# The Fourier stage of an encoder trunk, feature transform first: from transposed input through a transpose on TensorE to the token transform

## The chip, the cores and the metric

The kernel runs on one core of a Trainium2 chip. Its engines are TensorE (PE; PEld is its weight load), VectorE (DVE), ScalarE (ACT), GpSimd (POOL) and SyncE (SP, which here only issues DMAs). The metric is the device time of one execution in microseconds (us); lower is better. The profile is one execution taken by the hardware profiler; "span" is the time from its first to its last instruction.

## What is computed

Two sequences of 512 tokens and 1024 features go through the same two layers. The part that matters is the token mixer of layer 0, a Fourier mixing over tokens and, in eight groups of 128, over features:

```python
def rms_norm(x, g):
    x32 = x.astype(jnp.float32)
    y = x32 * lax.rsqrt(jnp.mean(x32 * x32, axis=-1, keepdims=True) + EPS)
    return (y * g.astype(jnp.float32)).astype(x.dtype)

def fourier_mix(h, w_out):
    B, S, _ = h.shape
    hg = h.astype(jnp.float32).reshape(B, S, N_FGROUPS, F_GROUP)
    f = jnp.fft.fft2(hg, axes=(1, 3), norm="ortho").real
    f = f.reshape(B, S, D_MODEL).astype(h.dtype)
    return f @ w_out
...
x = x + fourier_mix(rms_norm(x, fourier_norm[j]), fourier_w_out[j])
```

The real part of the two-dimensional transform is cosine times cosine minus sine times sine. Behind it, layer 0 has a squared-ReLU MLP, layer 1 has attention and another MLP, and a final norm ends the trunk; none of that is touched.

## The kernel before

**Precision.** Every matmul operand is split into a rounded part (hi, float32r) and the rest (lo). `split` (L80) does it with a cast on ACT and a subtraction on DVE (or POOL), `split_scaled` (L84) with a scale on the way. `mm3` (L75) makes a product from three matmuls: hi·hi, hi·lo, lo·hi (lines L76, L77 and L78 of the profile).

**Buffers.** All large tiles share 38 slots of 4 KB a partition (`slot`), eight of 2 KB (`tm`), five raw load buffers (`rawp`), four weight pairs (`wp`) and the eight PSUM banks (`ps`). The order of all five queues in the Fourier stage is the order of the calls in the program (`manual_schedule`): an instruction that waits holds up everything behind it on its own engine.

**The Fourier stage before.** Each input comes twice: as `x` by tokens ([token, feature], tokens and features folded so that mirrored ones lie together) for the transform, and as `xt` transposed for the residual. Per sequence:

- `Front` (L325) takes two of the four token tiles: sum of squares on ACT, gain on DVE (L339), sum and difference of mirrored features (`plus`, `minus`), root of the norm, scale by it, fold of mirrored tokens (`combine`), split. `mask` and row 0 carry token 256, which has no mirror.
- `transform` (L443) runs the token transform first (`seq_part`, L403: cosine and sine tables as the moving operand, 258 or 256 columns), evacuates and splits it (`seq_evac`), and then the feature transform (`feat_stage`, L419). The middle feature (64 of a group) goes beside it: 8-row operands (`seq_nyq`, `nyqT`), and the alternating row for token 256 is a product with one row (L395, L396).
- `even_outs` and `odd_outs` (L518 to L538) multiply the two halves of the result by folded output weights, four tiles `we` and four tiles `wo`, made by `Fold` (L462: plus, minus, even, odd) and, for the middle features, `FoldNyq`. Each output group is 12 matmuls, in the even half with one more for the middle features (L532).

The order (L578 on): Front of sequence 0, its transform with the weight folds on POOL in between, loads of the next `x`, then even and odd outputs of sequence 0 while Front of sequence 1 runs. As `xt` of sequence 0 isn't yet needed, `Aside` (L551) copies these outputs off by ACT and adds them to `xt` later, on POOL and DVE, during sequence 1's transform. Then come the outputs of sequence 1, added at once (`even_add`, `odd_add`), beside which the next stage begins: squares and gains of sequence 0 (`finish`), its root, and the first MLP weights.

**The lines of the steps.** `sums` (L156) adds squares over the partitions by float32 matmuls against a tile of ones (L160); `spread` and `tokens` show a float32 transpose on TensorE (L168, L1344). `rsqrt_steps` (L121) is a chain of seven small steps over DVE and ACT.

Of the kernel before, what the change touches and what calls it, by code (L numbers as in the profile page):

```python
# [11 lines left out]
F32 = mybir.dt.float32  # L12
# [6 lines left out]
P = 128  # L19
D = 1024  # L20
# [19 lines left out]
def trunk_kernel(ctx, tc, x_in, xt_in, y_out, dcos, dsin, feat, rope, gfour, gcol, grow, gfin,  # L40
# [215 lines left out]
    xa = {}  # L256

    def load_x(q, t):
        xa[q, t] = slot([P, D], F32)
        nc.sync.dma_start(xa[q, t], x_in[q][t * P : (t + 1) * P, :])  # L260

# [11 lines left out]
    def begin():  # L273
        gr = slot([P, D], F32)
        nc.sync.dma_start(gr, gfour.to_broadcast([P, D]))
        load_x(0, 0)
        load_x(0, 1)
        rcos = table(dcos, 3 * 258)
        load_x(0, 2)
        load_x(0, 3)  # L280
        rsin = table(dsin, 512)
        rft = table(feat, 846)
        gc = cons.tile([P, 4 * KC], F32, name="gc")
        nc.sync.dma_start(gc, gcol)
        return gr, rcos, rsin, rft, gc
# [11 lines left out]
    gr, rcos, rsin, rft, gc = begin()  # L297
    tabs = [slot([P, D], F32R) for _ in range(2)]
    cosT = [t[:, :516].rearrange("p (a b) -> p a b", a=2) for t in tabs]
    altT = tabs[0][0:1, 516:774]  # L300
    pickT = tabs[1][:, 516:594]
    sinT = slot([P, 2, 512], F32R)
    fslot = slot([P, D], F32R)
    ft = fslot[:, :512].rearrange("p (a b) -> p a b", a=2)
    nyqT = fslot[0:8, 512:1024]

    def table_cos():
        for c in range(2):
            split(cosT[c][:, 0], cosT[c][:, 1], rcos[:, c * 258 : (c + 1) * 258])
        nc.scalar.copy(altT, rcos[0:1, 516:774])  # L310
# [4 lines left out]
    def table_feat():  # L315
        split(ft[:, 0], ft[:, 1], rft[:, :256])
        nc.scalar.copy(nyqT, rft[0:8, 334:846])
        nc.scalar.copy(pickT, rft[:, 256:334])
# [4 lines left out]
    ee, oo, ny = {}, {}, {}  # L323

    class Front:  # L325


        def __init__(self, q, c):
            self.q, self.c = q, c
            self.ss, self.r = small(2), small(2)  # L330
            self.steps = rsqrt_steps(self.r[:, :2], self.ss[:, :2], 2, 1.0 / D)
            self.xg, self.p, self.m = [None] * 2, [None] * 2, [None] * 2

        def squares(self, i):
            sumsq(xa[self.q, 2 * self.c + i], self.ss[:, i : i + 1])

        def gain(self, i):
            self.xg[i] = slot([P, D], F32)
            nc.vector.tensor_mul(self.xg[i], xa[self.q, 2 * self.c + i], gr)  # L339

        def plus(self, i):
            self.p[i] = tm()
            nc.vector.tensor_add(self.p[i], self.xg[i][:, :512], self.xg[i][:, 512:])

        def minus(self, i):
            self.m[i] = tm()
            nc.vector.tensor_sub(self.m[i], self.xg[i][:, :512], self.xg[i][:, 512:])

        def chain(self, a, b):
            for step in self.steps[a:b]:  # L350
                step()
            if b == 7 and self.c == 0:
                self.rm = small(1)
                nc.vector.tensor_mul(self.rm[:, :1], self.r[:, 1:2], mask)

        def scale(self):
            for x in (self.m[0], self.p[0]):
                nc.scalar.activation(x, x, AF.Copy, scale=self.r[:, 0:1])

        def combine(self):  # L360
            (p1, p2), (m1, m2), r, w = self.p, self.m, self.r, 8
            stt = nc.vector.scalar_tensor_tensor
            n32 = sm.tile([P, 16], F32, tag="n32", name=nm("n32"), bufs=2)
            n = sm.tile([P, 2, 16], F32R, tag="ny", name=nm("ny"), bufs=4)


            rr = r[:, 1:2]
            if self.c == 0:
                rr, w = self.rm[:, :1], 16
                nc.vector.tensor_scalar(n32[:, 8:16], m2[:, 0:512:64], r[:, 1:2], None, ALU.mult)  # L370
            stt(n32[:, 0:8], m2[:, 0:512:64], rr, m1[:, 0:512:64], ALU.mult, ALU.add)
            stt(p1, p2, rr, p1, ALU.mult, ALU.add)
            stt(m2, m2, r[:, 1:2], m1, ALU.mult, ALU.subtract)
            split(n[:, 0, :w], n[:, 1, :w], n32[:, :w])
            ny[self.q, self.c] = n

        def split_even(self):
            e = slot([P, 2, 512], F32R)
            split(e[:, 0], e[:, 1], self.p[0])
            ee[self.q, self.c] = e  # L380

        def split_odd(self, eng=nc.vector):
            o = slot([P, 2, 512], F32R)
            if self.c == 0:
                nc.scalar.activation(self.m[1][0:1, :], self.p[1][0:1, :], AF.Copy, scale=self.r[0:1, 1:2])
            split(o[:, 0], o[:, 1], self.m[1], eng)
            oo[self.q, self.c] = o

        def split(self, eng=nc.vector):
            self.split_even()  # L390
            self.split_odd(eng)

    def seq_even(o, lhs, alt, c):
        if c == 1:
            nc.tensor.matmul(o, alt[0], altT, start=False, stop=False)  # L395
            nc.tensor.matmul(o, alt[1], altT, start=False, stop=False)  # L396
        mm3(o, lhs[0], lhs[1], cosT[c][:, 0], cosT[c][:, 1], c == 0, c == 1)

    def seq_nyq(q, c, o):
        seq_even(o[0:8, :258], [ny[q, c][:, i, 0:8] for i in range(2)],  # L400
                 [ny[q, 0][0:1, i, 8:16] for i in range(2)], c)

    def seq_part(q, j, c, o, v):  # L403
        js = slice(j * P, (j + 1) * P)
        seq_even(o[:, :258], [ee[q, c][:, i, js] for i in range(2)],
                 [oo[q, 0][0:1, i, js] for i in range(2)], c)
        cs = slice(c * 256, (c + 1) * 256)
        mm3(v[:, :256], oo[q, c][:, 0, js], oo[q, c][:, 1, js],
            sinT[:, 0, cs], sinT[:, 1, cs], c == 0, c == 1)

    def seq_evac(o, v):
        a, b = slot([P, 2, 258], F32R), tm((P, 2, 256), F32R)
        split(a[:, 0], a[:, 1], o[:, :258])
        split(b[:, 0], b[:, 1], v[:, :256])
        return a, b
# [3 lines left out]
    def feat_stage(q, j, a, b, an, en):  # L419
        u, v = ps(), ps()  # L420
        mm3(u[:, :258], ft[:, 0, 0:P], ft[:, 1, 0:P], a[:, 0], a[:, 1], True, False)
        nyt = nyqT[:, j * P : (j + 1) * P]
        nc.tensor.matmul(u[:, :258], nyt, an[0:8, 0], start=False, stop=False)
        nc.tensor.matmul(u[:, :258], nyt, an[0:8, 1], start=False, stop=True)
        mm3(v[:, :256], ft[:, 0, P:], ft[:, 1, P:], b[:, 0], b[:, 1], True, True)
        ent = pickT[:, 6 - 2 * j : 78 - 2 * j]
        nc.tensor.matmul(en[0:72, :258], ent, a[:, 0], start=j == 0, stop=False)
        nc.tensor.matmul(en[0:72, :258], ent, a[:, 1], start=False, stop=j == 3)
        t = slot([P, 2, 512], F32R)
        split(t[:, 0, 0:257], t[:, 1, 0:257], u[:, :257])  # L430
        split(t[:, 0, 257:], t[:, 1, 257:], v[:, 1:256])
        uv[q, j] = t

    def nyq_out(q, en):
        t = slot([P, 258], F32R)[0:72]
        nc.scalar.copy(t, en[0:72, :258])
        nc.vector.tensor_sub(t[64:72], en[64:72, :258], f32(t[64:72]))
        un[q] = t

    def transform(q, mid=lambda: None, between=lambda j: None):  # L440
        on, ov = ps(), [(ps(), ps()) for _ in range(3)]
        seq_nyq(q, 0, on)
        for j in range(3):  # L443
            seq_part(q, j, 0, *ov[j])
        mid()
        en = ps()
        seq_nyq(q, 1, on)
        an = slot([P, 2, 258], F32R)
        split(an[0:8, 0], an[0:8, 1], on[0:8, :258])
        ab = []  # L450
        for j in range(3):
            seq_part(q, j, 1, *ov[j])
            ab.append(seq_evac(*ov[j]))
        between(0)
        feat_stage(q, 0, *ab[0], an, en)
        o3 = ps(), ps()
        for c in range(2):
            seq_part(q, 3, c, *o3)
        between(1)
        feat_stage(q, 1, *ab[1], an, en)  # L460
        ab.append(seq_evac(*o3))
        between(2)  # L462
        feat_stage(q, 2, *ab[2], an, en)
        between(3)
        feat_stage(q, 3, *ab[3], an, en)
        nyq_out(q, en)
# [84 lines left out]
    class Aside:  # L551


        def __init__(self, q, odd):
            self.q, self.odd, self.t, self.c = q, odd, [], None if odd else small(KC)
# [993 lines left out]
```

## Time and profile before

| | us |
|---|---|
| Median of 3 runs | 1784.64 |
| Lowest and highest | 1781.79, 1785.09 |
| Profiled execution | 1783.47 |
| Its span | 1781.7 |
| First matmul after the span's start | 14.85 |
| First output product of sequence 1 | 101.97 |

The page of the profile gives each engine's busy time, the span in 40 equal slices (busy share in tenths, granted TensorE clock in tenths of full speed), and groups of equal instructions. A row of a group reads: line, engine, operation, output<-input, shapes, count, then busy us and mean ns of one, then the idle time ahead of them and what ended it. A row of the timeline reads: start, duration, engine, line, operation. Matmuls overlap, so the cost of one in a stream is the distance from start to start, not its duration.

### The profile page before, as it was taken

What the parts mean: (1) busy time and instruction counts of PE and PEld (TensorE: products, weight loads), DVE (VectorE), ACT (ScalarE), POOL (GpSimd) and SP (SyncE); (2) the same over time, 40 slices, a digit from 0 to 9 for tenths busy, and PEclk for the clock granted to TensorE, in tenths of its full rate; (3) what the DMA queues carried; (4) which work ended last, traced back from release to release, by engine and by line L of the source; (5) the groups of instructions that cost most, each with busy time, mean ns of one, the idle gap of its engine ahead of it and who ended that gap; (6) DMA issues with size and microseconds to landing.
All of it is one profiled execution on the core that took longest, in us unless ns stands there. A gap on an engine that the chain in (4) does not pass through costs nothing. (4 is left out here: it accounts for less than half of the span.)

```text
span 1781.7 us, 22113 instructions
## 1 busy us (share of the span) xinstructions
PE 1722.3 (97%) x7918; PEld 1417.7 (80%) x7918; DVE 1225.2 (69%) x1777; ACT 867.0 (49%) x1531; POOL 478.4 (27%) x382
## 2 busy tenths in 40 slices
PE   5999999999999999999999999999999999999997
PEld 4887877887778778878877888787788877878777
DVE  6867777455787686666578853687845478686765
ACT  4556545445534242345687733564544554343234
POOL 3550143223221111243334302204332232111103
PEclk7889999999999999999999999999999999999999
DMA  7234355337865353431100122224544486364232
GB/s 279 102 119 136 113 184 198 144 136 265 286 199 195 130 183 101 166 124 48 48 24 1 49 94 107 95 95 180 204 154 148 182 320 230 128 224 163 99 107 95
DMA packets 101670, 260.83 MB, mean 146 GB/s; under 512 B 10024, under 2 KB 10024, under 8 KB 101560
## 3 DMA queue, kind: packets, MB, share of 16 engines
q1 hardware_dynamic: 87160, 233.20, 37.4%
q10 hardware_dynamic: 14400, 26.22, 3.9%
q8 instruction: 62, 1.02, 0.2%
q14 instruction: 48, 0.39, 0.1%
HBM read 187.03 MB, written 72.35 MB: 146 GB/s over the span
## 5 line engine op out<-in xcount | busy, mean ns | idle before, releaser
L748 PE MATMUL ps<-u,w 128*128 128x512 f32 x4752 | 1094.6, 391 | 14.6 <-DVE u L960 8.0
L748 PEld LDWEIGHTS ps<-u,w 128*128 128x128 f32 x4752 | 889.0, 188 | 213.3 <-issue 9.3
L81 ACT CAST w<-raw 128x1024 fp32r<-128x1024 f32 (+2 forms) x250 | 232.0, 932 | 488.5 <-PE ps L748 299.4
L82 DVE TENSOR_TENSOR w<-raw,w 128x1024 fp32r<-128x1024 f32 (+2 forms) x246 | 274.1, 1117 | 65.7 <-ACT w L81 64.9
L82 DVE TENSOR_TENSOR u<-u,u 128x1024 fp32r<-128x1024 f32 x122 | 162.3, 1346 | 25.4 <-ACT u L81 25.2
L960 DVE TENSOR_TENSOR u<-ps,u 128x512 f32<-128x512 f32 x160 | 109.7, 687 | 97.8 <-PE ps L748 97.2
L81 ACT CAST u<-u 128x1024 fp32r<-128x1024 f32 x123 | 126.5, 1050 | 81.6 <-DMA u<-spill_b 61.9
L851 POOL TENSOR_TENSOR u<-u 128x512 f32<-128x512 f32 x28 | 38.3, 1367 | 446.2 <-ACT u L762 446.2
L1005 POOL TENSOR_TENSOR raw<-raw,raw 128x512 f32<-128x512 f32 (+1 forms) x32 | 43.4, 1356 | 419.0 <-DVE raw L1004 376.2
L76 PE MATMUL ps<-u,u 128*128 128x512 f32 (+2 forms) x392 | 153.2, 393 | 2.4 <-ACT u L561 1.6
L77 PE MATMUL ps<-u,u 128*128 128x512 f32 (+2 forms) x392 | 147.2, 376 | 1.5 <-DVE u L82 1.5
L78 PE MATMUL ps<-u,u 128*128 128x512 f32 (+2 forms) x392 | 147.2, 375 | 0.6 <-POOL u L82 0.6
L154 POOL TENSOR_TENSOR t<-t,t 128x512 f32<-128x512 f32 (+1 forms) x56 | 75.8, 1354 | 213.6 <-ACT t L152 153.8
L82 DVE TENSOR_TENSOR u<-ps,u 128x512 fp32r<-128x512 f32 (+4 forms) x126 | 76.6, 627 | 23.9 <-ACT u L81 22.8
L76 PE MATMUL ps<-u,w 128*128 128x512 f32 (+2 forms) x256 | 91.4, 357 | 0.9 <-ACT w L81 0.9
L732 DVE TENSOR_TENSOR u<-ps,u 128x512 f32<-128x512 f32 (+1 forms) x64 | 41.9, 656 | 72.7 <-PE ps L78 72.7
L78 PE MATMUL ps<-u,w 128*128 128x512 f32 (+2 forms) x256 | 90.8, 356 | 0.5 <-DVE w L82 0.5
L77 PE MATMUL ps<-u,w 128*128 128x512 f32 (+2 forms) x256 | 90.8, 355 | 0.0
L76 PEld LDWEIGHTS ps<-u,u 128*128 128x128 f32 x392 | 78.7, 201 | 15.1 <-ACT u L81 2.5
L77 PEld LDWEIGHTS ps<-u,u 128*128 128x128 f32 x392 | 79.1, 202 | 13.1 <-DVE u L82 4.2
L748 PE MATMUL ps<-u,u 128*128 128x512 f32 x336 | 82.0, 393 | 7.6 <-DVE t L829 7.6
L78 PEld LDWEIGHTS ps<-u,u 128*128 128x128 f32 x392 | 78.6, 201 | 12.8 <-POOL u L82 0.8
(210 smaller groups left out, 2141.9 us busy)
## 6 DMA issues: line engine op xcount, KB each, us to landing
raw<-w_up SPq DMA_DIRECT2D x84, 512.0 KB, 4.0
u<-spill_t SPq DMA_DIRECT2D x56, 512.0 KB, 6.6
raw<-w_sum SPq DMA_DIRECT2D x48, 512.0 KB, 3.6
spill_t<-u SPq DMA_DIRECT2D x84, 256.0 KB, 2.0
u<-spill_b SPq DMA_DIRECT2D x42, 512.0 KB, 5.8
spill_b<-t ACTq DMA_DIRECT2D x56, 256.0 KB, 2.0
park<-u SPq DMA_DIRECT2D x24, 512.0 KB, 2.6
raw<-w_row SPq DMA_DIRECT2D x24, 512.0 KB, 3.4
```

What stands on the lines that cost most here:

```text
L76: nc.tensor.matmul(out, lh, rh, start=first, stop=False)
L77: nc.tensor.matmul(out, lh, rl, start=False, stop=False)
L78: nc.tensor.matmul(out, ll, rh, start=False, stop=last)
L81: nc.scalar.copy(dst_hi, src)
L82: eng.tensor_sub(dst_lo, src, f32(dst_hi))
L154: nc.gpsimd.tensor_add(acc[q][:, :n], acc[q][:, :n], s[:, :n])
L732: nc.vector.tensor_add(x[:, :n], o[:, :n], x[:, :n])
L748: nc.tensor.matmul(o, w[x][:, sl], h[k][y], start=first and k + i == 0, stop=k == n - 1 and i == 2, skip_group_check=not first)
L851: nc.gpsimd.tensor_sub(t[:, 0], b12, b11)
L960: nc.vector.tensor_add(x, o, x)
L1005: nc.gpsimd.tensor_sub(a11, a11, a21)
```

## The change

The input comes only transposed (`xt`); the loads by tokens, the gain by rows, `Front`, `transform` and `Aside` go. A class `Mix` does the stage in the other order: each of the eight feature groups is scaled by the gain (now a column) and split, goes through the feature transform as the moving operand, is transposed on TensorE group by group into eight PSUM banks, is scaled there by the norm's root, folded over mirrored tokens and split, and goes through the token transform, whose result is what the outputs take. The middle feature rides along in column 0 of each sine half. The sums of squares come from 32 float32 matmuls per sequence. The alternating row `altT` now has all 128 partitions. Two small loads move to ACT's queue; all weights of the fold are asked for at once.

```diff
     def begin():
-        gr = slot([P, D], F32)
-        nc.sync.dma_start(gr, gfour.to_broadcast([P, D]))
-        load_x(0, 0)
...
+        gc = cons.tile([P, 5 * KC], F32, name="gc")
+        nc.scalar.dma_start(gc, gcol)
+        rft = rawp.tile([P, 256], F32, tag="raw", name=nm("raw"))
+        nc.scalar.dma_start(rft, feat)
+        load_xs(0, xt_in[0])
+        rcos, rsin = table(dcos, 3 * 258), table(dsin, 512)
+        load_xs(1, xt_in[1])
+        return gc, rft, rcos, rsin
...
+    class Mix:
...
+        def halves(self, fo, eng=None):
+            h, g = slot([P, 2, 512], F32R), gc[:, 4 * KC + fo : 4 * KC + fo + 1]
+            if eng is None:
+                split_scaled(h[:, 0], h[:, 1], xt(self.q, fo), g)
+            else:
+                eng.tensor_scalar(h[:, 0], xt(self.q, fo), g, None, ALU.mult)
+                eng.scalar_tensor_tensor(h[:, 1], xt(self.q, fo), g, f32(h[:, 0]), ALU.mult, ALU.subtract)
+            self.x[fo] = h
...
+        def feature(self, g, move=nc.scalar.copy):
+            o, x = ps(), self.x[g]
+            for i in range(2):
+                c = slice(i * 256, (i + 1) * 256)
+                mm3(o[:, c], ft[:, 0, i], ft[:, 1, i], x[:, 0, c], x[:, 1, c], True, True)
+            if g % 2 == 0:
+                self.y[g // 2] = slot([P, 2, 512], F32)
+            move(self.y[g // 2][:, g % 2], o)
+
+        def turn(self, g, ts=range(4)):
+            for t in ts:
+                nc.tensor.transpose(self.bank(t, g // 4)[:, g % 4 * P : (g % 4 + 1) * P],
+                                    self.y[g // 2][:, g % 2, cols(t)], ident)
+
+        def sums(self, fo):
+
+            o = self.bank(3, 1)
+            for t in range(NT):
+                nc.tensor.matmul(o[:, 2 * t : 2 * t + 2], self.sq[fo][:, cols(t)], ones, start=fo + t == 0,
+                                 stop=fo + t == KC + NT - 2, skip_group_check=True)
...
+        def scale(self, c, h):
+            self.s[c, h] = tm()
+            nc.scalar.activation(self.s[c, h], self.o[2 * c, h], AF.Copy, scale=self.r[:, 2 * c : 2 * c + 1])
+
+        def fold(self, c, h):
+
+
+            t, r = 2 * c + 1, self.r[:, 2 * c + 1 : 2 * c + 2]
+            s = self.s[c, h]
+            nc.vector.scalar_tensor_tensor(s, self.o[t, h], self.rm[:, :1] if c == 0 else r, s, ALU.mult, ALU.add)
...
+        def seq(self, j):
+            self.ov[j] = o, v = ps(), ps()
+            js = slice(j * P, (j + 1) * P)
+            for c in range(2):
+                hl = self.hi[c], self.lo[c]
+                self.even(o[:, :258], [x[:, 0, js] for x in hl], [x[:, 1, js] for x in (self.hi[0], self.lo[0])], c)
+                cs = slice(c * 256, (c + 1) * 256)
+                mm3(v[:, :256], hl[0][:, 1, js], hl[1][:, 1, js], sinT[:, 0, cs], sinT[:, 1, cs], c == 0, c == 1)
...
+        for i in range(4):
+            m0.halves(2 * i)
+            m0.halves(2 * i + 1, vec)
+            m0.square(2 * i)
+            m0.square(2 * i + 1, gps if i < 3 else None)
+            if i:
+                m0.feature(2 * i - 2)
+                m0.feature(2 * i - 1)
+        for g in (6, 7):
+            m0.feature(g, vec.tensor_copy)
+        for g in range(4):
+            m0.turn(g)
+        for fo in range(KC):
+            m0.sums(fo)
+        for fo in range(2):
+            m1.halves(fo, vec)
+        m0.root()
+        for g in range(2):
+            m1.feature(g)
+        for g in range(4, KC):
+            m0.turn(g)
         table_cos()
         table_sin()
+        m0.room()
...
+        folded(m0)
+        for f in fold:
+            f.plus(gps)
+        for j in range(3):
+            m0.seq(j)
+        m0.middle()
+        m0.seq(3)
+        for j in range(4):
+            m0.out(j)
+            if j < 3:
+                m1.halves(2 + 2 * j)
+                m1.halves(3 + 2 * j, vec)
+            m1.square(2 * j)
+            m1.square(2 * j + 1)
+        m0.out_middle()
+        for g in range(2, KC):
+            m1.feature(g)
+        for g in range(4):
+            m1.turn(g)
+        for fo in range(KC):
+            m1.sums(fo)
+        m1.root()
+        for g in range(4, KC):
+            m1.turn(g)
+        for f in fold:
+            f.minus()
+        for f in fold[:2]:
+            f.even()
+        wn.combine()
+        wn.hi()
+        wn.lo()
+        m1.room()
...
+        folded(m1)
+        for f in fold[2:]:
+            f.even()
+        o = even_outs(0, range(4))
+        for fo in range(4):
+            even_add(0, fo, o[fo])
+        for j in range(3):
+            m1.seq(j)
+        m1.middle()
+        m1.seq(3)
+        for f in fold:
+            f.odd()
+        for j in range(4):
+            m1.out(j)
+        m1.out_middle()
+        for fo, o in zip(range(4, KC), even_outs(0, range(4, KC))):
+            even_add(0, fo, o)
+        for fos in (range(i, i + 2) for i in range(0, KC, 2)):
+            for fo, o in zip(fos, odd_outs(0, fos)):
+                odd_add(0, fo, o)
         raws = [load_raw(w_up[0, 2 * p]) for p in range(4)]
```

`root` runs the first step of the root chain, straight from the sums in PSUM, and leaves the others to `folded`. `folded` runs these, then for both token halves (c) and both feature halves (h) `scale`, `fold` (with small strided copies for the middle features), the splits of the result, and the splits of the middle rows. `middle` is the token transform of the middle features (8 matmuls), `out` splits its result into the tiles `uv` that the output products take.

More of the change, by code (lines that the diff above doesn't have):

```diff
@@ L393, in seq_even @@
[L393 to L409, printed above, removed]
@@ L434, in nyq_out @@
[L434 to L466, printed above, removed]
+        split(ft[:, 0].rearrange("p a b -> p (a b)"), ft[:, 1].rearrange("p a b -> p (a b)"), rft)
```

350 lines of the change are left out of this document (105 added, 245 removed).

## The prediction

> **What bounds the kernel now.** I began with the page: the span, the engines' busy time, and the forty slices with the granted clock.
>
> ```profile
> span 1781.7 us, 22113 instructions
> PE 1722.3 (97%) x7918; PEld 1417.7 (80%) x7918; DVE 1225.2 (69%) x1777; ACT 867.0 (49%) x1531; POOL 478.4 (27%) x382
> PE   5999999999999999999999999999999999999997
> PEclk7889999999999999999999999999999999999999
> ```
>
> TensorE (PE) is busy for 97% of the span, so the time is what TensorE is given to do, at the clock it is granted, plus its few idle stretches. The first slices hold both exceptions: a half-idle start and a clock of 0.7 to 0.9. That is where the Fourier stage lies, so I next cut it into windows of 10 us (columns: sum, PE, PEld, DVE, ACT, POOL, clock, DMA share, GB/s).
>
> ```profile
> 0.00:10.00 10.00, 0.00 (x0) 0.00 (x0) 3.61 (x8) 3.78 (x6) 0.70 (x6) 1.00 0.80 291
> 10.00:20.00 10.00, 4.08 (x13) 2.55 (x14) 8.01 (x22) 7.82 (x18) 0.00 (x0) 1.00 1.03 406
> 30.00:40.00 10.00, 10.00 (x38) 8.64 (x39) 6.50 (x9) 4.13 (x8) 10.00 (x5) 0.50 0.35 130
> 40.00:50.00 10.00, 10.00 (x41) 8.63 (x40) 8.96 (x12) 7.42 (x14) 3.15 (x2) 0.50 0.31 107
> 80.00:90.00 10.00, 10.00 (x38) 7.91 (x38) 5.43 (x12) 3.77 (x11) 9.08 (x9) 0.51 0.01 2
> ```
>
> TensorE waits for the load and the norm at first, and then runs both transforms at half clock. The stage has clear marks in TensorE's timeline (columns: start, duration, then the instruction).
>
> ```profile
> 14.85 0.38 PE L76 MATMUL ps<-u,ny 128*8 128x258 f32 x1 [14.85 <-ACT ny L81]
> ...
> 48.24 0.42 PE L76 MATMUL ps<-u,w 128*128 128x258 f32 x1
> ...
> 53.04 0.28 PE L78 MATMUL ps<-u,w 128*128 128x258 f32 x1
> 53.16 0.28 PE L76 MATMUL ps<-u,w 128*128 128x258 f32 x1
> ...
> 75.15 0.28 PE L76 MATMUL ps<-u,ny 128*8 128x258 f32 x1
> ...
> 101.97 0.42 PE L76 MATMUL ps<-u,w 128*128 128x258 f32 x1
> ...
> 104.10 0.28 PE L77 MATMUL ps<-u,w 128*128 128x258 f32 x1
> ```
>
> First matmul at 14.85; sequence 0's output products at 48.24; sequence 1's transform at 75.15 and its output products at 101.97. From 101.97 on the code is the same in both kernels, so the forecast is 1783.47 us (the profiled execution; span 1781.7, 1.8 around it) plus the shift of that one matmul. The median of the runs shown, 1784.64, lies 1.2 above that execution, which is inside their spread.
>
> **The change part by part.** Removed: eight loads by tokens and the gain's (4.5 MB), the wait until 14.85, the Aside copies, and the matmuls of 1 and 8 rows. Added per sequence: 48 feature matmuls of 256 columns for 40, 32 transposes, 32 sums of squares by float32 matmul, and a scale-and-fold between the two transforms. The matmul of about 256 columns goes every 0.12 us at full clock (53.04 to 53.16) and every 0.21 at half, as here:
>
> ```profile
> 79.61 0.28 PE L395 MATMUL ps<-u,ny 1*8 1x258 f32 x1
> 79.73 0.28 PE L396 MATMUL ps<-u,ny 1*8 1x258 f32 x1
> 79.94 0.28 PE L76 MATMUL ps<-u,ny 128*8 128x258 f32 x1
> ...
> 82.94 0.58 PE L395 MATMUL ps<-u,u 1*128 1x258 f32 x1
> 83.33 0.41 PE L396 MATMUL ps<-u,u 1*128 1x258 f32 x1
> 83.67 0.58 PE L76 MATMUL ps<-u,u 128*128 128x258 f32 x1
> 84.05 0.42 PE L77 MATMUL ps<-u,u 128*128 128x258 f32 x1
> 84.26 0.42 PE L78 MATMUL ps<-u,u 128*128 128x258 f32 x1
> ```
>
> Where the row count switches, a weight load is laid bare: 0.09 us beyond the pace at full clock (79.73 to 79.94), 0.13 to 0.17 at half (83.33 to 83.67, 83.67 to 84.05). Weight loads therefore slow down with the clock by about half. Transposes and sums are bound by them. Their rows, all at full clock:
>
> ```profile
> 137.84 0.95 PE L160 MATMUL ps<-ones,t 128*128 128x2 f32 x8
> 138.65 2.58 PE L748 MATMUL ps<-u,w 128*128 128x512 f32 x10
> ...
> 1745.12 1.91 PE L1344 MATMUL ps<-ident,u 128*128 128x128 f32 x16
> 1746.78 0.36 PE L76 MATMUL ps<-u,w 128*128 128x256 f32 x1
> ```
>
> Four sums take 0.81 us, 0.20 each; sixteen transposes 1.66, 0.104 each. At half clock nothing here shows them: from 0.20 (no slowing) to 0.40 (double) for a sum. I take 0.31 and 0.155, the ratio of the bared weight loads. The prices of the other engines:
>
> ```profile
> L372 DVE SCALAR_TENSOR_TENSOR t<-t,s,t 128x512 f32<-128x512 f32 x4 | 3.0, 751 | 0.8 <-ACT t L358 0.7
> L1414 DVE TENSOR_SCALAR u<-u,s 128x512 f32<-128x512 f32 x1 | 0.5, 488 | 0.1
> L82 DVE TENSOR_TENSOR u<-t,u 128x512 fp32r<-128x512 f32 x6 | 4.2, 692 | 1.6 <-ACT u L81 1.6
> L82 DVE TENSOR_TENSOR w<-raw,w 128x1024 fp32r<-128x1024 f32 x2 | 2.4, 1224 | 0.6 <-ACT w L81 0.6
> L490 DVE TENSOR_TENSOR w<-u,w 128x1024 fp32r<-128x1024 f32 x4 | 8.6, 2158 | 0.5 <-ACT w L486 0.5
> L128 DVE RECIPROCAL s<-s 128x2 f32<-128x2 f32 x4 | 0.6, 160 | 0.3 <-ACT s L127 0.3
> L358 ACT ACTIVATE t<-t,s 128x512 f32<-128x512 f32 x8 | 5.3, 714 | 4.6 <-DVE s L132 4.6
> L169 ACT COPY t<-ps 128x512 f32<-128x512 f32 x1 | 0.6, 567 | 0.0
> L486 ACT CAST w<-u 128x1024 fp32r<-128x1024 f32 x4 | 4.1, 1058 | 0.0
> u<-gfour SPq DMA_DIRECT2D x1, 512.0 KB, 4.3
> ```
>
> L490 against L82 is the same subtraction with GpSimd (POOL) at work beside it: 2.16 for 1.22. Now the walk, each step ending at a time of the new kernel:
>
> 1. The first 512 KB land 4.3 us after issue, the table on ACT's queue a little later; split and first halves end about 6.2. DVE then has eight corrections at 0.75 and four scalings at 0.49, 8 us, and about 1 us more while POOL squares. TensorE's last feature transform follows: **16.5**. By then TensorE has been dense for some 8 us at half clock, so I count full clock here.
> 2. Sixteen transposes 1.7; 32 sums, during which the multiplier idles and the clock should fall: 21 at 0.20, 11 at 0.31, 7.6. **25.8**.
> 3. Sequence 1's first two feature transforms stand ahead, 12 matmuls at half clock 2.6; behind their copies (0.6) ACT splits the cosine and sine tables (four casts, by L358 and its like 1.8), and then come the root's seven remaining steps (0.16 and a handover each, 1.5): **32.3**. The other 16 transposes are hidden here.
> 4. Scale, fold, split until both halves of the tokens are there: one scale 0.7; three folds on DVE at 0.75 with 0.3 of small copies each, 3.15; two corrections at 0.69, made 1.2 by POOL's weight folds beside them, 2.4; handovers and what ACT does between, 1.05 as an allowance: 7.3. TensorE idles for most of it: **39.6**.
> 5. 58 matmuls of the token transform, 24 at half clock until it lifts (5 us), 34 at full: 9.2. **48.8**.
> 6. Six feature transforms of sequence 1, 36 matmuls, 4.3 (the halves on DVE hold them only slightly, 0.1): **53.2**.
> 7. Transposes and sums again 9.3: **62.5**. The squares were made by ACT beside step 5.
> 8. DVE and ACT now split two weights (2.4), combine, round and correct the middle row's (1.2, 1.05, 1.2) ahead of the root's remaining steps (1.3), all queued behind the root's first step, which waited for the sums. Only the last 16 transposes (2.5) cover any of it: **69.7**.
> 9. The whole fold, without POOL: one scale 0.7, four folds 4.2, four corrections 2.8, the middle row's small splits 0.5, handovers 1.3, in all 9.5. TensorE can do half of four output products in it, then waits until weights 2 are split (1.06 and 1.22, begun a little earlier), 1.7: **80.9**.
> 10. Rest of those products 3.2; 64 transform matmuls, 52 and 96 of the output products at 0.12, 25.4: **109.5**.
>
> The shift is 109.5 - 101.97 = +7.5. Before, ten matmuls from 101.97 to 104.10 ran at half clock; that 0.9 goes. So 1783.47 + 6.6 = **1790** us. The dropped loads cost nothing at this end: no wait for data is left after step 1. POOL's folds are free where TensorE is not waiting for DVE; in step 4 they are in the 7.3.
>
> **Bounds.** The 22 sums at half clock: 2.4 less with no slowing, 2.0 more with double; 3.7 more if the clock is low from step 1 on, so that all of step 2 runs at half. The clock's lift in step 5: at once 2.3 less, not at all 3.1 more, and 8.7 more if it stays low through sequence 1's 92 matmuls as well. POOL beside the folds: 1.2 less to 3 more. Load at the start: 1 either way.
>
> Weighed against a rule: the Trainium skill, TensorE: Matmul & The Clock Gate, section "LDWEIGHTS (loading the stationary operand)", gives the number of columns divided by 1.2 as a load's ns, 107 ns for 128, and names no dependence on the gate; by it the sums would be 0.20 throughout. The rows above speak against it, 0.09 at full clock to 0.13 to 0.17 at half. The same page, "The HAM clock gate", has the clock lift after a busy window of about 3.4 us; in the windows from 30 to 50 us it stayed at 0.50 with PE at 10.00 of 10.00, so what counts as busy must be stricter than the profile's busy time.
>
> **The rivals.**
> A. Weight loads don't slow at half clock: 2.4 go, and the clock holds until step 3 is through, 1.1: 3.5 less, 1786.5 us, no change that could be told. For it: transposes do move 128 columns. Against it: the bared loads.
> B. The clock stays low: the token transform is no more "busy" than the old one was, and steps 5, 9 and 10 run at half clock up to the output products: 6.6 + 3.1 + 8.7 = 18.4, 1802 us. For it: two transforms of more than 20 us without a lift. Against it: those were broken every few matmuls by bared weight loads, and the dense products behind them were at full clock within 4.9 us and 2.1 us (48.24 to 53.16, 101.97 to 104.10).
> C. The other side: not slower. The clock, once up in step 1, isn't lost until sequence 0's transform is done, because transposes and loads count as activity. The sums save 2.4, step 3's features 1.1, step 5 saves 2.3: 5.8, 1784 us; with the lower bounds of the folds (1.2) and of the start (1) beside it 1782, and 1780 where the handovers overlap too (2.3). It decides if the 32 sums of sequence 0 take under 6.6 us and its token transform begins at full clock. For it: the first matmul comes some 8 us before 14.85, and the 1-row matmuls are gone. Against it: a sum moves two columns, and waiting this short halved the clock before (it was 0.50 from about 26 us on):
>
> ```profile
> 25.26 0.29 PE L76 MATMUL ps<-u,ny 128*8 128x258 f32 x1 [2.80 <-ACT ny L81]
> 26.00:28.00 2.00, 1.43 (x5) 0.97 (x6) 1.57 (x4) 1.31 (x3) 0.82 (x1) 0.50 1.00 365
> ```
>
> **How the numbers follow.** The forecast, 1790, has 0.46; A 0.11; B 0.15; C 0.28. A difference under 0.2% (3.6 us) can't be told from none in this kernel. Against 1784.64, the forecast's and B's outcomes are slower, 0.61; A is within it, and so is C with the smaller of its savings, 0.11 each, together 0.22; C with the larger ones is faster, 0.17. The forecast's own range is 1786 to 1796. The whole reaches down to C's full saving, 1780, and up to 1800, just under B's price, which the bounds on sums, folds and step 5 together could also reach; about 2 in 10 are left out.
>
> **What would show it.** Right: first matmul near 7 us; sums at 0.2 to 0.31 each, some 7 to 8 us per sequence in which DVE waits; TensorE idle for 5 us or more ahead of each token transform; 1.00 clock through sequence 1's transform; the first output products of sequence 1 near 109. Step 8 is right if DVE's weight splits stand between the sums and the root's square root. Wrong: clock 0.5 through the second transform (B), sums at 0.20 everywhere (A), or that first output product before 102 (C). My whole reading would be wrong if the difference arose behind it.

## The result and the profile after

The changed kernel takes **1800.3 us** (median of four runs, 1799.1 to 1803.1), the kernel before 1783.7 beside it: a ratio of 1.0097, 95% interval 1.0081 to 1.0113. It is slower, as forecast, but by 16.6 us instead of 6.6, and it ends just beyond the range, which stopped at 1800. The profiled execution is one of 1799.96 us.

The first lines of the page:

```profile
span 1798.1 us, 22508 instructions
PE 1735.7 (97%) x8126; PEld 1439.6 (80%) x8126; DVE 1211.9 (67%) x1784; ACT 865.3 (48%) x1505; POOL 465.3 (26%) x376
PEclk7799999999999999999999999999999999999999
```

The share of TensorE is the same as before, 97%, and only the first two slices of the clock differ from full. So the loss lies in the first 90 us. The windows of 10 us (columns as before: sum, PE, PEld, DVE, ACT, POOL, clock, DMA share, GB/s):

```profile
20.00:30.00 10.00, 10.00 (x59) 10.00 (x59) 1.07 (x2) 0.00 (x0) 8.66 (x6) 0.62 0.71 261
30.00:40.00 10.00, 6.54 (x32) 5.90 (x31) 5.71 (x4) 2.72 (x7) 10.00 (x5) 0.67 0.05 17
40.00:50.00 10.00, 3.98 (x14) 3.23 (x15) 7.22 (x20) 5.11 (x10) 0.63 (x1) 0.50 0.25 89
80.00:90.00 10.00, 5.59 (x24) 5.08 (x24) 7.17 (x21) 5.88 (x13) 0.00 (x0) 0.66 0.00 0
```

Before, TensorE was slow but full between 30 and 50 us and between 80 and 90; now it stands idle for half of those stretches. From 20 to 30 it is full, with sums, and there VectorE has almost nothing to do and ScalarE nothing. TensorE's timeline, at the marks of the ten steps:

```profile
7.49 0.58 PE L76 MATMUL ps<-u,u 128*128 128x256 f32 x1 [7.49 <-ACT u L85]
...
17.85 1.91 PE L359 MATMUL ps<-ident,u 128*128 128x128 f32 x16
...
47.41 0.42 PE L416 MATMUL ps<-u,u 128*128 128x258 f32 x1
...
57.43 0.28 PE L76 MATMUL ps<-u,u 128*128 128x256 f32 x1
...
61.74 1.91 PE L359 MATMUL ps<-ident,u 128*128 128x128 f32 x16
...
82.12 0.58 PE L76 MATMUL ps<-u,w 128*128 128x258 f32 x1 [4.72 <-ACT t L387]
...
92.25 0.58 PE L78 MATMUL ps<-u,w 128*128 128x258 f32 x1 [0.46 <-DVE w L470]
...
97.77 0.29 PE L76 MATMUL ps<-u,u 128*128 128x258 f32 x1
...
123.22 0.28 PE L76 MATMUL ps<-u,w 128*128 128x258 f32 x1
...
129.02 0.65 PE L512 MATMUL ps<-u,u 72*128 72x258 f32 x4
```

The first output product of sequence 1 starts at 123.22, where the forecast had 109.5 and the kernel before 101.97. (The row at 129.02, the middle row's products for the first four outputs, stands 5.80 us behind it; I read the same mark in the experiments.) Between 30 and 45 us the cause is on VectorE and GpSimd:

```profile
30.75 0.16 DVE L126 TENSOR_SCALAR s<-ps 128x4 f32<-128x4 f32 x1 [9.65 <-PE ps L366]
34.45 6.73 DVE L82 TENSOR_TENSOR u<-raw,u 128x258 fp32r<-128x258 f32 x3 [3.53 <-ACT u L81]
...
42.09 0.16 DVE L371 TENSOR_TENSOR s<-s,mask 128x1 f32<-128x1 f32 x1
...
30.96 7.18 POOL L462 TENSOR_TENSOR raw<-raw,u 128x1024 f32<-128x1024 f32 x3
38.11 2.52 POOL L462 TENSOR_TENSOR u<-u,u 128x1024 f32<-128x1024 f32 x1
```

Three small subtractions, the low parts of the cosine and sine tables, take 6.73 us. Beside nearly all of it, until 40.6, GpSimd forms the differences of the weights. The root's steps stand behind the three in VectorE's queue, and TensorE stands behind the root.

Behind the mark the two kernels run alike, and the shift can be followed in the stops of TensorE's timeline, the kernel before first:

```profile
130.60 1.91 PE L748 MATMUL ps<-u,w 128*128 128x512 f32 x5 [1.78 <-DVE u L223]
...
426.34 3.02 PE L748 MATMUL ps<-u,u 128*128 128x512 f32 x12 [1.66 <-DVE t L829]
...
1724.46 0.50 PE L76 MATMUL ps<-u,w 128*128 128x512 f32 x1 [0.91 <-ACT w L81]
```

The first and the last of these stops in the changed kernel's timeline:

```profile
150.97 5.30 PE L694 MATMUL ps<-u,w 128*128 128x512 f32 x15 [1.77 <-DVE u L223]
...
1740.94 0.50 PE L76 MATMUL ps<-u,w 128*128 128x512 f32 x1 [0.91 <-ACT w L81]
```

And a window of 4 us of each, behind a stop that both have (before at 774, after at 793):

```profile
776.00:780.00 4.00, 4.00 (x15) 3.33 (x15) 2.08 (x12) 1.39 (x4) 2.36 (x1) 0.57 0.82 231
```

```profile
796.00:800.00 4.00, 4.00 (x19) 3.29 (x18) 2.98 (x16) 2.37 (x5) 1.91 (x1) 1.00 0.68 234
```

The shift is 20.4 us at the first stop and 16.5 at the last. Some 3.4 of the 3.9 between have a place: the stop of 1.66 us at 426.34 has no counterpart after, and behind the other stop the clock fell before (0.57 over 4 us, 1.7 us lost) and not after. I take this for scatter rather than an effect of the change, which is not shown beyond this: in the experiments' traces such a fall comes and goes behind the same stop (e4 and e6 have it, the others don't), and the time behind the mark stays within 4 us (the table at their end).

### The profile page after: what moved, and what is told of

It reads as the page before. It is cut to its first block, busy times and chain, and to the rows that moved or that the text cites. A ratio compares the mean times of both kernels' runs of the same rounds, so it can differ in the third digit from the quotient of the medians.

```text
span 1798.1 us, 22508 instructions
## 1 busy us (share of the span) xinstructions
PE 1735.7 (97%) x8126; PEld 1439.6 (80%) x8126; DVE 1211.9 (67%) x1784; ACT 865.3 (48%) x1505; POOL 465.3 (26%) x376
## 5 line engine op out<-in xcount | busy, mean ns | idle before, releaser
L76 PE MATMUL ps<-u,u 128*128 128x512 f32 (+3 forms) x420 | 157.6, 377 | 17.1 <-ACT u L81 9.5
L77 PE MATMUL ps<-u,u 128*128 128x512 f32 (+3 forms) x420 | 153.6, 366 | 3.4 <-DVE u L82 1.6
L78 PE MATMUL ps<-u,u 128*128 128x512 f32 (+3 forms) x420 | 152.6, 363 | 0.0
L76 PEld LDWEIGHTS ps<-u,u 128*128 128x128 f32 (+1 forms) x420 | 82.0, 195 | 27.6 <-ACT u L81 10.7
L77 PEld LDWEIGHTS ps<-u,u 128*128 128x128 f32 (+1 forms) x420 | 81.8, 195 | 16.2 <-DVE u L82 4.3
L78 PEld LDWEIGHTS ps<-u,u 128*128 128x128 f32 (+1 forms) x420 | 81.4, 194 | 11.7 <-DVE u L82 0.5
L694 PEld LDWEIGHTS ps<-u,u 128*128 128x128 f32 x336 | 62.4, 188 | 22.0 <-issue 5.3
```

Of the source, the lines that this page charges most:

```text
L76: nc.tensor.matmul(out, lh, rh, start=first, stop=False)
L77: nc.tensor.matmul(out, lh, rl, start=False, stop=False)
L78: nc.tensor.matmul(out, ll, rh, start=False, stop=last)
L694: nc.tensor.matmul(o, w[x][:, sl], h[k][y], start=first and k + i == 0, stop=k == n - 1 and i == 2, skip_group_check=not first)
```

## Experiments

All start from the changed kernel, and the diffs are against it unless they name another.

**e1: the table splits out of the way.**

```diff
         for g in (6, 7):
             m0.feature(g, vec.tensor_copy)
+        table_cos()
+        table_sin()
...
-        table_cos()
-        table_sin()
         m0.room()
```

> The cosine and sine tables are split right after sequence 0's last feature transform instead of behind the sums. Theory (root held): in the changed kernel the root's remaining steps stand behind these splits on DVE, three subtractions of 6.7 us beside GpSimd, so the root was ready at 42.25 instead of about 36. Expected: root ready near 36, first output product of sequence 1 at 117 to 119 instead of 123.2, time 4 to 6 us less, 1794 to 1796. Rival (contention only moves): GpSimd still folds weights until 40.6, so the fold's own subtractions take the loss: 2 us less or none, 1798 to 1800.

1800.5 us, a ratio to the kernel before of 1.0097 (1.0065 to 1.0129): nothing gained, as the rival had it. Its timeline on VectorE and GpSimd:

```profile
18.38 1.36 DVE L82 TENSOR_TENSOR u<-raw,u 128x258 fp32r<-128x258 f32 x3
...
33.02 0.18 DVE L128 RECIPROCAL s<-s 128x4 f32<-128x4 f32 x1 [3.33 <-ACT s L127]
...
33.94 2.27 DVE L130 TENSOR_TENSOR s<-s,s 128x4 f32<-128x4 f32 x1
...
31.53 6.95 POOL L462 TENSOR_TENSOR raw<-raw,u 128x1024 f32<-128x1024 f32 x3
```

The three subtractions take 1.36 us where GpSimd does nothing, for 6.73 beside it: the price was the neighbour's. But the root's steps, now first in the queue, meet the same neighbour, and a step over four numbers per partition takes 2.27 us for 0.16. That is a whole GpSimd instruction (6.95 / 3 = 2.32). The root is ready at 41.0 instead of 42.25.

**e4: GpSimd out of the way.** The differences of the weights are queued behind the tiles of the second sequence, whose clearing waits for that sequence's sums.

```diff
-        for f in fold:
-            f.minus()
         for f in fold[:2]:
             f.even()
...
         m1.room()
+        for f in fold:
+            f.minus()
```

> GpSimd's four subtractions of weights (31 to 40.6 us) come behind the middle rows' buffers of sequence 1, so after 64 us; everything else in place. Theory (contention): the three table subtractions on DVE take about 2 us instead of 6.7, and the root is ready near 37.5 instead of 42.25: 4 to 5 us less, 1795 us, less what GpSimd then takes from DVE's weight splits near 75 us (up to 2). Rival (order alone, DVE slow by itself): the three keep their 6.7 us, 1800 us.

1797.1 us, 1.0080 (1.0048 to 1.0111). VectorE's timeline:

```profile
28.83 0.16 DVE L126 TENSOR_SCALAR s<-ps 128x4 f32<-128x4 f32 x1 [7.24 <-PE ps L366]
...
33.66 0.69 DVE L82 TENSOR_TENSOR u<-raw,u 128x512 fp32r<-128x512 f32 x1 [0.37 <-ACT u L81]
...
35.26 0.16 DVE L371 TENSOR_TENSOR s<-s,mask 128x1 f32<-128x1 f32 x1
```

The splits are back to their own size and the root is ready at 35.4, 6.8 us sooner, of which 1.9 had come about ahead of the root (28.83 for 30.75). From the sums' end (28.65) to the root it is 6.8 us where the changed kernel takes 11.7, so GpSimd costs 4.9 of them. The mark moves by 6.8 too, to 116.4; the time by only 3.2, and in the profiled execution 1.7 us go behind the mark to a fall of the clock (0.76 from 788 to 792 and 0.81 from 792 to 796) that the changed kernel's hasn't. So the contention is shown where it stands, and what it costs in all is settled by the mark better than by one kernel's time.

**e2: the weights split ahead of the second sequence's sums.**

```diff
         for g in range(2, KC):
             m1.feature(g)
+        for f in fold:
+            f.even()
+        wn.combine()
+        wn.hi()
+        wn.lo()
         for g in range(4):
             m1.turn(g)
```

(and the same calls are left out at their two places behind the root).

> All four even weights and the middle row's weight are split behind sequence 1's feature transforms, ahead of its root's first step, so while DVE waits for the sums (60 to 74 us). Theory (order on DVE): 5.9 us go ahead of the fold and the 2.4 behind it, TensorE no longer stops between the products of weights 1 and 2, and the clock comes back earlier: first output product of sequence 1 near 111 instead of 123.2, 1788 us. Rival (the fold is the bound): TensorE then waits for ACT and DVE in the fold of sequence 1 instead, only the 5.9 are gained: 1794 us.

1789.4 us, 1.0031 (1.0017 to 1.0046), and the mark at 109.9. From its timeline:

```profile
63.35 4.63 DVE L470 TENSOR_TENSOR w<-u,w 128x1024 fp32r<-128x1024 f32 x4 [3.02 <-ACT w L466]
...
74.23 0.16 DVE L126 TENSOR_SCALAR s<-ps 128x4 f32<-128x4 f32 x1 [2.76 <-PE ps L366]
...
77.36 0.56 PE L76 MATMUL ps<-u,w 128*128 128x258 f32 x1
```

Four splits fit where VectorE waited for sums, the root follows the sums at once, and TensorE reaches the first output product at 77.36 instead of 82.12, with no stop after it. This one order was worth 10.9 us: steps 8, 9 and the slow start of 10.

**e3: four sums instead of 32 per sequence.**

```diff
-        for fo in range(KC):
-            m0.sums(fo)
+        m0.sums(0)
```

(the same for the second sequence).

> Only the squares of the first 128 features are summed, 4 sums per sequence instead of 32 (the norm is then wrong). Theory (sums lie bare on the path): 28 of 32 sums at 0.34 go in each sequence, 9.6 and 9.2 us; the tables and GpSimd's folds give 1 to 2 back: 17 us less, 1783 us, with the first output product of sequence 1 near 106. Rival (something else is late next, the table split and the weight splits on DVE, whose loads or partners aren't there earlier): 8 to 10 us less, 1791 us.

1787.1 us, 1.0024 (1.0009 to 1.0038); the mark at 110.6, between the two expectations. The second sequence gave its 10 us; the first gave only 2.3 at its root, and the timeline shows why:

```profile
18.13 2.36 POOL L459 TENSOR_TENSOR u<-raw,u 128x1024 f32<-128x1024 f32 x1 [9.35 <-PE ps L78]
...
18.66 2.12 DVE L329 TENSOR_SCALAR u<-u,gc 128x512 fp32r<-128x512 f32 x1
20.81 2.77 DVE L330 SCALAR_TENSOR_TENSOR u<-u,gc,u 128x512 fp32r<-128x512 f32 x1
```

With the squares freed early GpSimd starts at 18.1 instead of 21.75, and now VectorE's halves are held: 2.12 to 2.77 us instead of the 0.48 and 0.75 that they take alone.

**e5: the same sums at half the price.** The squares and the ones are written as float32r.

```diff
-            self.sq[fo] = tm()
+            self.sq[fo] = tm((P, 512), F32R)
...
-                nc.tensor.matmul(o[:, 2 * t : 2 * t + 2], self.sq[fo][:, cols(t)], ones, ...
+                nc.tensor.matmul(o[:, 2 * t : 2 * t + 2], self.sq[fo][:, cols(t)], ones_r, ...
```

> One edit to the changed kernel: the squares, and the column of ones they are multiplied by, are written as float32r, so the 64 sum matmuls load their 128x128 weights in the rounded form (the mean square is then a sum of rounded squares). Theory, that a sum costs 0.36 us at half clock because its float32 weights are loaded in two bared passes: a sum falls to 0.10 to 0.18, the two groups of 32 from 11.0 and 10.5 us to 3 to 6 each. The second group's gain stays whole (-5 to -7); the first is in part eaten, because the GpSimd folds start as soon as the squares are freed and stand beside the steps of the root, as with four sums. Time 1786 to 1792. Rival, that the price is one of the instruction or of the one bank they all add to, not of the weights: a sum stays above 0.30 and the time at 1798 to 1802.

1792.3 us, 1.0046 (1.0031 to 1.0061), 0.3 above the range that was expected. The first sums of the changed kernel, in two stretches with the row that follows, and then a stretch of the second sums of this kernel (the count is of matmul passes):

```profile
19.59 2.85 PE L366 MATMUL ps<-ones,t 128*128 128x2 f32 x25
...
22.30 8.41 PE L366 MATMUL ps<-ones,t 128*128 128x2 f32 x39
30.58 0.56 PE L76 MATMUL ps<-u,u 128*128 128x256 f32 x1
```

```profile
63.67 2.27 PE L368 MATMUL ps<-ones_r,t 128*128 128x2 f32 x10
```

From start to start, 25 passes take 2.71 us in the changed kernel, 0.11 each, while the clock is at 1.00; the other 39 take 8.28, 0.21 each, nearly all of them at 0.50. In this kernel the next row starts at 65.80, so ten passes at 0.50 take 2.13 us, again 0.21 each. A pass thus costs 0.11 us at full clock and 0.21 at half, in either type. The float32 sum makes two passes, 64 for 32 sums, the float32r sum one. The price is that of the passes, as the theory had it. The first group's gain was again eaten, for the most part, by GpSimd: its sums end 7 us sooner (the root's first step comes at 23.70 for 30.75) and its root is ready only 1.5 sooner (40.75), as the table splits take 6.14 us there.

**e6: e2 and e4 together.**

```diff
+        for f in fold:
+            f.even()
         ...
         for g in range(4):
             m1.turn(g)
...
         m1.room()
+        for f in fold:
+            f.minus()
```

> The weights split early and the folds' differences behind the second sequence's tiles, together, in the changed kernel. Theory, that the two are separate waits: the gains add, 10.9 + 3.2 below 1800.3, so 1785 to 1788, first output of sequence 1 near 104. Rival, that GpSimd's differences, which then run at about 58 to 68, stand beside the weight splits and the second root: a VectorE split of 128x1024 takes 2.3 us there instead of 1.2, and the time is that of the weights alone, 1788 to 1793.

1788.8 us, 1.0025 (1.0015 to 1.0036), within a microsecond of e2 alone, the mark 1.4 earlier. The rival held:

```profile
57.80 8.94 DVE L470 TENSOR_TENSOR w<-u,w 128x1024 fp32r<-128x1024 f32 x4 [3.02 <-ACT w L466]
...
73.33 0.16 DVE L126 TENSOR_SCALAR s<-ps 128x4 f32<-128x4 f32 x1
```

The differences, moved away from the first root, now stand beside the weight splits: 8.94 us for 4.63, so 2.2 for each split. The second sums begin 5.4 us sooner than in e2 (57.5 for 62.9), and at the second root 0.9 of it is left (73.33 for 74.23).

**e7: sums in float32r, weights early, and all of GpSimd's folds late.** The low parts of the middle-row tile go to GpSimd, so that its queue waits for each fold; the four sums of weights then follow the first, the four differences the second.

```diff
-            split(self.ny[:, c, 0, :n], self.ny[:, c, 1, :n], self.n[c][:, :n])
+            split(self.ny[:, c, 0, :n], self.ny[:, c, 1, :n], self.n[c][:, :n], nc.gpsimd)
...
         folded(m1)
+        for f in fold:
+            f.minus()
```

> The three causes taken out of the changed kernel at once: sums in float32r, the weights split ahead of the second sums, and GpSimd's folds held back: it does the low parts of the small middle-row tile, which come last in each fold, so that its four sums start behind the first fold and its four differences behind the second. Theory: the first root is ready near 29 instead of 42, the second near 56 instead of 81, the first output of sequence 1 comes near 86 to 93 where the kernel before has 101.97, and the time is 1769 to 1777, below the kernel before. Rival, that GpSimd's sums now stand beside VectorE's halves of the second sequence and hold them, each for a 2.3 us instruction: the second feature transforms start up to 8 us later, and the time is 1778 to 1785.

1786.1 us, 1.0017 (1.0008 to 1.0025). The first root is ready at 28.6, as expected; then the rival came, and the time lies 1.1 above its range:

```profile
38.42 2.66 DVE L86 SCALAR_TENSOR_TENSOR u<-u,gc,u 128x512 fp32r<-128x512 f32 x1
...
46.32 0.41 DVE L82 TENSOR_TENSOR u<-ps,u 128x257 fp32r<-128x257 f32 x1
...
87.13 0.58 PE L76 MATMUL ps<-u,u 128*128 128x256 f32 x1 [5.94 <-DVE u L82]
```

VectorE's halves of the second sequence are held one GpSimd instruction each. The instruction at 46.32, which has one input in PSUM, isn't held, though GpSimd works beside it. The stop at 87.13 comes from GpSimd too, but by another way, a plain wait: ScalarE's casts of the odd weights wait for GpSimd's late differences, and the outputs of the second transform are queued behind them.

**e8: e7 with the first sums between the feature matmuls.** They go into a bank of their own, and the root's first step moves ahead of the transposes.

```diff
                 m0.feature(2 * i - 1)
+                m0.sums(2 * i - 2)
+                m0.sums(2 * i - 1)
```

> As the kernel with all three causes taken out, and the first sequence's sums put between its feature matmuls, into a bank of their own, with the root's first step ahead of the transposes. Theory, that TensorE waits for the tiles there (about 4 us idle of the 10 between 7.5 and 17.9) and the clock is still full: the sums cost nothing, the root is ready 3 us earlier, the time is 2 to 4 us below that of the kernel with the sums behind the transposes. Rival, that the root then meets other work (the copies and the table splits) before its 0.16 us steps can go: no gain, within 1 us of it.

1788.9 us, 1.0032 (1.0022 to 1.0042): 2.8 us worse than e7, with the mark 2.2 later, against both expectations. TensorE had no room there:

```profile
13.16 0.41 PE L77 MATMUL ps<-u,u 128*128 128x256 f32 x1
13.37 0.41 PE L78 MATMUL ps<-u,u 128*128 128x256 f32 x1
```

```profile
12.00:17.00 5.00, 5.00 (x25) 5.00 (x25) 1.92 (x4) 3.04 (x7) 0.44 (x2) 1.00 1.03 410
```

The matmuls go every 0.21 us, the pace of half clock, and TensorE is full. The clock column says 1.00 there; I had believed it. The pace of 0.12 comes only at 21.0 us, where the changed kernel has it from 12.2.

**e9: the folds on VectorE.** Float32r sums, weights early, tables early, and the eight folds on VectorE where it waits; GpSimd keeps half of the odd weights' low parts.

```diff
-            nc.gpsimd.tensor_sub(self.a, self.a, self.b)
+            nc.vector.tensor_sub(self.a, self.a, self.b)
...
-            split(hi, lo, self.a, nc.gpsimd)
+            split(hi, lo, self.a, nc.gpsimd if self.j % 2 else nc.vector)
...
+        fold[0].plus(vec)
+        wn.combine()
         m0.root()
```

> A version meant to keep all three gains: sums in float32r, weights split early, table splits right behind the first features, and the eight folds of the weights taken from GpSimd to VectorE, at places where VectorE waits (one sum and the middle row's difference ahead of the first root, three sums ahead of the weight splits, the differences behind the second fold); GpSimd keeps half of the low parts of the odd weights. Theory, that the time is lost in VectorE's steps held for whole GpSimd instructions, and that a fold costs VectorE 1.2 us where it delays nobody: first root ready near 26, second near 55, first output of sequence 1 near 86 to 92, time 1768 to 1775. Rival, that VectorE has no such room (eight folds are 9.4 us): its weight splits and the second root come as late as with the folds on GpSimd, and the time is 1780 to 1786, no better than the kernel before.

1775.7 us, 0.9961 (0.9949 to 0.9973): faster than the kernel before, and 24.7 us below the changed one. The mark and the time miss the expected ranges, the time by 0.7, and the first root is later than expected, 32.6; one row tells why:

```profile
29.83 1.22 DVE L489 TENSOR_TENSOR u<-u,u 72x1024 f32<-72x1024 f32 x1 [6.56 <-DMA u<-w_nyq]
```

The middle row's difference, which I had put ahead of the root, waits for its load.

**e10: e9 with that difference behind the halves.**

```diff
-        fold[0].plus(vec)
-        wn.combine()
+        for f in fold[:2]:
+            f.plus(vec)
         m0.root()
```

> As the version without GpSimd's folds, but the middle row's difference, which stood in VectorE's queue ahead of the first root and waited 6.56 us there for its load, goes behind the second sequence's halves, and the second fold's sum takes its place. Theory, that this wait is all that holds the first root: it is ready near 26 instead of 32.4, the first token transform starts 5 to 6 us earlier, and the time falls by 3 to 6 us, to 1769.5 to 1773. Rival, that VectorE's later queue (two sums, the difference, four weight splits, the middle row's split) then decides when the second root comes, because it can't start before the second sequence's halves are done: the second root keeps its place within 2 us, and the time stays within 2 us of 1775.7.

**1770.6 us**, 0.9927 (0.9913 to 0.9940), the best version. The root is ready at 27.7, 4.9 us sooner than in e9, and the mark and the second root (56.8 for 61.7) move by as much: the theory held. Its timeline:

```profile
27.55 0.16 DVE L373 TENSOR_TENSOR s<-s,mask 128x1 f32<-128x1 f32 x1
...
98.89 0.65 PE L514 MATMUL ps<-u,u 72*128 72x258 f32 x4
```

All runs side by side; the mark is that of the row at 98.89 here and 129.02 in the changed kernel, less 5.80, in the profiled execution. The time is the median of the runs, and the last column is the time less the mark:

| kernel | first output product of sequence 1 | time, us | rest |
|---|---|---|---|
| changed | 123.2 | 1800.3 | 1677.1 |
| e1 tables early | 121.4 | 1800.5 | 1679.1 |
| e2 weights early | 109.9 | 1789.4 | 1679.5 |
| e3 four sums | 110.6 | 1787.1 | 1676.5 |
| e4 differences late | 116.4 | 1797.1 | 1680.7 |
| e5 float32r sums | 114.2 | 1792.3 | 1678.1 |
| e6 weights early, differences late | 108.5 | 1788.8 | 1680.3 |
| e7 all of it, folds on GpSimd late | 108.9 | 1786.1 | 1677.2 |
| e8 sums between | 111.2 | 1788.9 | 1677.7 |
| e9 folds on VectorE | 98.0 | 1775.7 | 1677.7 |
| e10 difference behind | 93.1 | 1770.6 | 1677.5 |

Over a span of 30 us of the mark the rest stays between 1676.5 and 1680.7. The stage decides, and what is behind it adds a scatter of 4 us, which is how e4 could lose half of its gain. For the kernel before, 1783.7 less 101.97 is 1681.7, of which 0.9 is the half clock at its mark.

## Why the forecast was right in direction and too small

The way of reckoning held: a walk through the steps to one mark, and the shift of that mark. By steps, forecast length against the length in the trace:

| step | forecast | measured | difference |
|---|---|---|---|
| 1 start and features | 16.5 | 17.85 | +1.35 |
| 2 transposes, sums | 9.3 | 12.7 | +3.4 |
| 3 until the root | 6.5 | 11.7 | +5.2 |
| 4 fold | 7.3 | 5.2 | -2.1 |
| 5 token transform | 9.2 | 10.0 | +0.8 |
| 6 features | 4.3 | 4.3 | 0 |
| 7 transposes, sums | 9.3 | 12.3 | +3.0 |
| 8 weights, root | 7.2 | 7.4 | +0.2 |
| 9 fold | 11.2 | 10.8 | -0.4 |
| 10 to the mark | 28.6 | 31.0 | +2.4 |

Steps 4 and 9 end at the rows at 47.41, where 58 of the 64 transform matmuls are left, and 92.25. Together +13.85, and the mark is 13.7 late (123.22 for 109.5). The 0.9 us that were to come back at full clock did: 21.25 at the mark is 20.4 at the first stop. That the time missed by 10 us and not by 13.7 is luck: 3.9 us of the shift went behind that stop, where the forecast had nothing.

**Step 3 failed.** The forecast put the table splits and the root at 6.5 us and saw GpSimd's folds only in step 4 ("made 1.2 by POOL's weight folds beside them"). They stood beside step 3 as well, and their price isn't a ratio. I had read it from one pair, 2.16 for 1.22, both of 1024 elements; e1 shows that an instruction of four elements is held just as long, 2.27 us. The trace before had shown that too, in its timeline at the second sequence's front:

```profile
57.96 2.87 DVE L343 TENSOR_TENSOR t<-u 128x512 f32<-128x512 f32 x1
60.75 2.89 DVE L347 TENSOR_TENSOR t<-u 128x512 f32<-128x512 f32 x1
...
60.24 2.84 POOL L82 TENSOR_TENSOR u<-raw,u 128x1024 fp32r<-128x1024 f32 x1
```

Half the elements of L490, and each as long as the GpSimd instruction beside it. By the Trainium skill, SBUF — State Buffer, section "Who interferes with whom", a VectorE instruction with two inputs in SBUF contends with a GpSimd instruction that reads SBUF, and one with at most one SBUF input, outside the two-port modes, doesn't; of those modes it says that whichever engine issues first holds the shared ports for its whole instruction, and the other is blocked. The runs agree: 2.27 us for two SBUF inputs, 0.41 for an input from PSUM (e7) and 0.18 for the reciprocal (e1). The same error has the other sign in step 4: most of its work reads PSUM and GpSimd had finished, so the allowances were too large by 2.1. The rest of step 3 was right: with GpSimd out of the way, in e4, it takes 6.8 us for the 6.5 forecast.

**Steps 2 and 7 were mis-sized.** The mechanism was right, passes that slow with the clock while the sums let the clock fall. The size wasn't: the prediction took "about half" from matmuls at which a load lies bare, and in the sums a pass goes from 0.11 to 0.21 us, nearly double. A sum at half clock costs 0.42 (two passes), not 0.31, beyond the upper bound of 0.40. And the clock fell sooner than after 21 sums: it averages 0.62 over the window from 20 to 30, which puts the fall at about 22.4, 2.8 us and some 12 sums behind the first. Together 6.4 us. When it falls is in part chance: the same 64 passes in the same place took 8.71 us in e4, 9.45 in e2 and 10.66 in e6, for 11.12 here.

**Step 10**: I let the output products begin at half clock but forgot that the stops of step 9 would keep it low: 5.5 us instead of 3.2 up to the dense run. The 212 matmuls took 25.45 us, as reckoned. Of step 1's 1.35 some part is scatter (the transposes begin between 17.6 and 18.3 in the kernels with the same start); the rest, and step 5's 0.8, I did not follow up.

**Steps 8 and 9 were right**, and with them the reading that weight splits queued between the sums and the root cost time: e2, which moves them, gains 10.9 us.

Of the rivals, A fell: sums don't stay at 0.20 (0.22 at full clock, 0.42 at half). B fell: the dense part of the second transform ran at 1.00. C fell in both its signs: the first sums took 11 us, and the first token transform began at half clock. C named the right place, though. The stage can be made to win, but by other means than a clock that holds: e10's gain comes from cheaper sums and from what VectorE waits for.

The range failed at its upper end because it allowed 3 us for GpSimd beside VectorE in one step and 2.0 for the price of the sums. And five of the six steps that were off by more than 1 us were off to the slow side, so that bounds meant as independent added up.

## What to carry to other kernels

Price a neighbour's contention by the neighbour's instruction, not by a ratio: put GpSimd's long instructions where VectorE works on PSUM or waits, and never beside a chain of short steps that TensorE waits for. When a serial step (sums, root, scale) is put between two transforms, fill the wait that it makes with work that stands behind it in the same queues, before adding any. Test such moves in pairs too: e4 and e2 each gained alone, and together hardly more than e2.

## What was unexpected of the hardware

A float32 matmul of two columns runs as two passes, each 0.11 us at full clock and 0.21 at half, and a float32r one as one pass of the same price. So a pass of two columns costs about what a matmul of 256 costs here (0.12 and 0.21), and half clock nearly doubles both. And in e8 the clock column reads 1.00 from the start of the span, while the matmuls go at the pace of half clock until 20 us (0.21 us); only behind that does it agree with the pace. In the changed kernel it is the same until 12 us. Whether the kernel before would gain as much from folds on VectorE was not tried; its trace has the same held instructions.
